# A decoder layer on one core: part of the weight and token sums of its seven-product groups move from accumulating DMAs and VectorE to GpSimd adds

## The chip, the core and the metric

One core of a Trainium2 chip runs the whole layer. The metric is the device time of one execution in microseconds; three executions of the kernel before gave 404.01, 404.17 and 405.35 us (median 404.17).

## What is computed

One decoder layer in float32 for 256 tokens of width 1024: a mixed attention block (block-sparse attention beside chunkwise retention), a cross-attention block over 256 memory rows, and a SwiGLU feed-forward block, each with RMS norms before and after. The change touches the last block alone:

```python
h = rms_norm(x, g_pre_ffn[l])
gu = h @ w_gate_up[l]
f = (jax.nn.silu(gu[..., :D_FF]) * gu[..., D_FF:]) @ w_down[l]
x = x + rms_norm(f, g_post_ffn[l])
```

`w_gate_up` is 1024 x 5632 and `w_down` 2816 x 1024.

## The kernel before

**Weights.** The host cuts all weights into blocks of 128 x 1024 floats (512 KB), here called quarters and numbered `q` in the order of their splitting. A quarter is loaded by one DMA of the SP queue into one of 5 `raw` buffers (L143). `split_weight` then splits it into two float32r matrices whose sum is the float32 value: ScalarE copies it rounded, the **high part** (L183), and VectorE subtracts that from the raw value, the **low part** (L184). TensorE multiplies with three products (high x high, high x low, low x high), for the operands on both sides are split so. Split quarters live in a ring of 9 `hl` buffers; while a quarter of the feed-forward stage finds no ring buffer free, `free_home` (L155) may also put it into the old activation tiles tagged "qv", "kT" and "ret": all three for the first 8 quarters of the stage, and after them "ret" alone.

**Order.** The program is written out step by step: a list `steps` of small groups of products sets TensorE's order, and after each step the loop emits what is due on the other engines: generators with waits counted in steps (table `WAIT`), and at most one split, once a home is free and, for a quarter that is a sum, at least `WAIT["sum"]` steps after the split of the value before it. Each engine works its own queue in that order.

**Seven-product groups.** Of the gate-up columns, two groups of 512 + 512 (`SEVEN = (2, 4)`, called group 2 and group 4) are computed as a 2 x 2 block product with seven products m1 to m7 instead of eight. The blocks are two token halves by two halves of the inner dimension, and B11, B12 (inner half 1, gate and up) and B21, B22 (inner half 2) for the weights. Each product takes two quarters. Its operands are sums: on the token side four sums per pair of inner blocks (`token_sums`, L602), made by VectorE from the normed tokens `x2T` (`xs`, `cs`: L612 to L619) and then split into `comb`; on the weight side sums that grow in place. In `seven_items` (L859) the tile `sum_kT` starts as B11 (weights of m1), becomes B11 + B12 (m5), + B22 (m6), + B21 (m4), and `sum_qv` starts as B22 (m3) and becomes B22 + B12 (m7). Each step on is an **accumulating DMA** of the GpSimd queue from the weights in HBM (L190), issued when the low part of the value before it has been read. The weights of m2, B21, are plain quarters. Between the seven products stand `down` products of earlier columns, one quarter each.

The quarters are used as `USE_ORDER` says: m1, d0, m2, d1, m5, d2, d3, m6, d4, m3, d5, m7, d6, m4, d7; they are split in the same order but for m3, which is split ahead of m6. In group 2 these are quarters 80 to 101: m1 is 80 and 81, m2 83 and 84, m5 86 and 87, m3 90 and 91, m6 92 and 93, m7 96 and 97, m4 99 and 100, the rest `down` quarters. Group 4 begins at 110 in the same way.

**After the products** (`seven_done`, L645): ScalarE copies the accumulators of m1, m5 and m6 (`s<-x`, `s<-y`); at m2 VectorE adds (`s<-z`, L651) and ScalarE applies silu (L653); at m3 VectorE computes `s<-y` (L656) and `s<-s` (L657), and two steps later TensorE transposes the result (`c_f`, L637) for the `down` products that follow.

Of the kernel before, what the change touches and what calls it, by code (L numbers as in the profile page):

```python
# [7 lines left out]
F32 = mybir.dt.float32  # L8
# [14 lines left out]
FFN_Q = 64  # L23
# [15 lines left out]
}  # L39
WARM = 9  # L40
# [7 lines left out]
def tile_hybrid_layer(  # L48
# [14 lines left out]
    nc = tc.nc  # L63
# [50 lines left out]
    T = {}  # L114
# [16 lines left out]
    items = [("w", q) for q in range(FFN_Q)]  # L131
    queue = []
    sums = {}
# [17 lines left out]
    homes = {}  # L151
# [2 lines left out]

    def free_home(q, i):  # L155

        if q in aside and last_use[homes["ret"]] + WAIT["lag"] <= i:
            return "ret"
        if len(ringed) < RING or last_use[ringed[-RING]] + WAIT["lag"] <= i:
            return "hl"  # L160
        if q >= FFN_Q and ("oT", 7, 1) in emitted:
            for tag in ("qv", "kT", "ret") if q < FFN_Q + 8 else ("ret",) if not any(q < a <= q + 6 for a in aside) else ():
                if tag not in homes or last_use[homes[tag]] + WAIT["lag"] <= i:
                    return tag
        return None

    def split_weight(q, parts=1, home="hl"):
        kind = items[q][0]
        if kind == "w":
            raw = raws.pop(q)  # L170
        else:
            g, tag, part = items[q][2:5]
            raw = sums[(g, tag)][:, part, :]
        if home == "hl":
            ringed.append(q)
            h = hlp.tile([P, 2, D], F32R, tag="hl", name=f"hl{q}")
        else:
            homes[home] = q
            h = actp.tile([P, 2, D], F32R, tag=home, name=f"hl{q}")
        w = D // parts  # L180
        for i in range(parts):
            n = slice(i * w, (i + 1) * w)
            nc.scalar.activation(h[:, 0, n], raw[:, n], AF.Copy)  # L183
            nc.vector.tensor_tensor(out=h[:, 1, n], in0=raw[:, n], in1=h[:, 0, n].bitcast(F32), op=ALU.subtract)  # L184
        hls[q] = h
        split_at[q] = step_no[0]
        if kind != "w":
            more = items[q][5]
            if more is not None:
                nc.gpsimd.dma_start(raw, weights[more], accum_op=ALU.add)  # L190
        if kind == "w":
            load_weight()

# [409 lines left out]
    def token_sums():  # L603

        T["comb"] = [(pt4 if i < 3 else p4).tile([P, 2, 4, P], F32R, tag="pt4" if i < 3 else "p4", name=f"comb{i}")
                     for i in range(4)]
        for i in range(4):
            need(*[("x2T", 2 * i + e, t) for e in range(2) for t in range(2)])
            x = tmp2k(f"xs{i}")
            pair = x.rearrange("p (e m) -> p e m", e=2)  # L610
            ks = slice(2 * i, 2 * i + 2)
            nc.vector.tensor_tensor(out=pair, in0=T["x2T"][:, 0, ks, :].bitcast(F32), in1=T["x2T"][:, 1, ks, :].bitcast(F32),  # L612
                                    op=ALU.add)
            c = tmp2k(f"cs{i}")
            nc.vector.tensor_tensor(out=c[:, 0:256].rearrange("p (e m) -> p e m", e=2),
                                    in0=x[:, 0:256].rearrange("p (e m) -> p e m", e=2), in1=pair[:, :, P:256],
                                    op=ALU.subtract)
            nc.vector.tensor_tensor(out=c[:, 256:384], in0=c[:, 128:256], in1=x[:, 0:P], op=ALU.subtract)
            nc.vector.tensor_tensor(out=c[:, 384:512], in0=c[:, 256:384], in1=x[:, 256:384], op=ALU.add)  # L619
            yield WAIT["ts0"]  # L620
            hi_lo(T["comb"][i][:, 0].rearrange("p c m -> p (c m)"), T["comb"][i][:, 1].rearrange("p c m -> p (c m)"), c)
            emitted.add(f"comb{i}")
            yield WAIT["ts1"]
# [235 lines left out]
    def seven_items(g, w0):  # L859

        b = {"11": w0, "12": w0 + 2, "21": w0 + 4, "22": w0 + 6}
        chain = {1: ("first", "11", "kT", "12"), 5: ("sum", "", "kT", "22"), 6: ("sum", "", "kT", "21"),
                 4: ("sum", "", "kT", None), 3: ("first", "22", "qv", "12"), 7: ("sum", "", "qv", None)}
        made = {}
        for m in range(1, 8):
            for part in range(2):
                if m == 2:
                    made[(m, part)] = ("w", b["21"] + part)
                else:
                    kind, w, home, more = chain[m]  # L870
                    made[(m, part)] = (kind, b[w] + part if w else None, g, home, part,
                                       None if more is None else b[more] + part)
        return made

    def seven_step(g, m, part, q):
# [1 line left out]
        begin = part == 0 and m in (1, 2, 5)  # L877
        steps.append(("seven", q, g, m, part, acc, begin))

    aside = set()  # L880
    for j in range(1, 5):
        if j not in SEVEN:
            gu_plain(range(4 * j, 4 * j + 4))
# [4 lines left out]
        made = seven_items(j, take(8)[0])  # L888
# [24 lines left out]
    last_use, first_use = {}, {}  # L913
# [6 lines left out]
    after = {}  # L920
    for q, item in enumerate(items):
        if item[0] == "sum":
            after[q] = max(p for p in range(q) if items[p][0] != "w" and items[p][2:5] == item[2:5])


    nc.gpsimd.memset(mhalf, -0.5)
# [11 lines left out]
    qv = actp.tile([P, 2048], F32, tag="qv", name="qv")  # L938
# [14 lines left out]
    nc.sync.dma_start(xr[0][:, 1, :], gx[:, 288:544])  # L953
    nc.sync.dma_start(raws[1][:, 512:1024], weights[1, :, 512:1024])
    nc.sync.dma_start(xr[0][:, 2:4, :], gx[:, 544:1056].rearrange("p (k m) -> p k m", k=2))
    queue[:] = [q for q in range(2, len(items)) if items[q][0] != "sum"]
    load_weight()
    load_weight()
    nc.sync.dma_start(xr[1], gx[:, 1056:2080].rearrange("p (k m) -> p k m", k=4))
# [49 lines left out]
    raw = raws.pop(0)  # L1009
# [19 lines left out]
    for i, s in enumerate(steps):  # L1029
# [17 lines left out]
        if s[0] == "first":  # L1047

            _, q, c = s
# [8 lines left out]
        elif s[0] == "col":  # L1058
            _, q, t, st, kp, key, first, last, done = s
# [15 lines left out]
        elif s[0] == "row":  # L1075
            _, q, half, st, nt, done = s
# [23 lines left out]
        elif s[0] == "down":  # L1100
            _, q, t, j, kk, halves = s
# [169 lines left out]
```

## Time and profile before

| | |
|---|---|
| three executions | 404.01, 404.17, 405.35 us (median 404.17) |
| the profiled execution | 404.76 us, of it 403.0 us span |
| granted TensorE clock | 0.997 |
| busy: TensorE / VectorE / ScalarE / GpSimd | 394.1 / 290.3 / 248.8 / 25.3 us |
| the chain that ended last | TensorE 71%, issue 9%, VectorE 6%, DMA 6%, ScalarE 4%, GpSimd 2% |
| DMA | 82.46 MB, mean 205 GB/s |
| feed-forward stage in the span | from about 215 us; group 2 from 261 to 304, group 4 from 326 to 368 |

The profile is of one execution. Engines are named PE (TensorE), PEld (its weight loads), DVE (VectorE), ACT (ScalarE), POOL (GpSimd), SP; a line L184 is that of the kernel before. A product's busy time overlaps the next one's, so TensorE's load is read from the distance of starts and from the idle time in brackets, not from its busy share. What an engine waits for matters where TensorE waits behind it.

### The profile page before, as it was taken

The numbers are of one execution on the slowest core, as the hardware profiler recorded it, in microseconds if no ns is written. First come the engines' busy times: TensorE is split into PE (matmuls) and PEld (weight loads), VectorE is DVE, ScalarE is ACT, GpSimd is POOL, SyncE is SP. The second block draws the span as 40 slices with busy tenths as digits, with TensorE's granted clock in tenths as the row PEclk, the third lists the DMA queues.
The fourth block names the chain that finished last, engine by engine and source line by source line (L and its number), as shares of the span: only waits on it lengthen the run. The fifth ranks groups of instructions, "written<-read, shape, count | busy, mean of one in ns | idle before, by whom it ended". The sixth has DMA issues, their size and how long they took to land.

```text
span 403.0 us, 5622 instructions
## 1 busy us (share of the span) xinstructions
PE 394.1 (98%) x2041; PEld 330.5 (82%) x2041; DVE 290.3 (72%) x435; ACT 248.8 (62%) x437; POOL 25.3 (6%) x37
## 2 busy tenths in 40 slices
PE   9999999999999999999999999999999999999993
PEld 5887777888888888988888888888788888878882
DVE  4885965776789977586656888888577667676732
ACT  5776883955667766485556865567365666664620
POOL 0010100200010000000011001013000103100000
PEclk9999999999999999999999999999999999999998
DMA  8998754387547676425354686989949798958011
GB/s 289 413 338 251 265 187 168 104 251 269 184 137 227 193 214 198 158 74 189 113 201 156 183 279 194 308 180 200 264 134 337 191 333 175 236 181 293 11 54 52
DMA packets 23499, 82.46 MB, mean 205 GB/s; under 512 B 2608, under 2 KB 2864, under 8 KB 23472
## 3 DMA queue, kind: packets, MB, share of 16 engines
q1 hardware_dynamic: 21024, 73.46, 53.5%
q0 software_dynamic: 2304, 8.39, 11.7%
q8 instruction: 16, 0.26, 0.3%
q10 hardware_dynamic: 144, 0.26, 0.2%
q14 instruction: 11, 0.09, 0.1%
HBM read 81.05 MB, written 1.05 MB: 204 GB/s over the span
## 4 chain that ended last, share of the span: by engine, by line
PE 71%; issue 9%; DVE 6%; DMA 6%; ACT 4%; POOL 2%; POOLq 0%; DVEq 0%; ACTq 0%
PE acc L1093 13%; PE acc L1069 10%; PE acc L1071 10%; PE acc L1070 10%; PE acc L1096 7%; DMA sum_kT<-in_weights_dram 6%; PE x L1129 3%; DVE hl L184 3%; PE acc L1057 3%; ACT hl L183 2%; PE down L1116 2%; PE down L1114 2%; PE down L1115 2%; PE warm L937 1%; ACT p_m L295 1%
## 5 line engine op out<-in xcount | busy, mean ns | idle before, releaser
L184 DVE TENSOR_TENSOR hl<-raw,hl 128x1024 fp32r<-128x1024 f32 (+1 forms) x120 | 140.7, 1194 | 25.3 <-ACT hl L183 24.9
L183 ACT ACTIVATE hl<-raw 128x1024 fp32r<-128x1024 f32 (+1 forms) x120 | 120.7, 1034 | 1.3 <-DMA raw<-in_weights_dram 1.2
L1093 PE MATMUL acc<-x2T,hl 128*128 128x512 f32 x160 | 39.2, 392 | 0.0
L1114 PE MATMUL down<-hl,fT 128*128 128x512 f32 x88 | 34.2, 389 | 0.0
L1115 PE MATMUL down<-hl,fT 128*128 128x512 f32 x88 | 34.2, 389 | 0.0
L1116 PE MATMUL down<-hl,fT 128*128 128x512 f32 x88 | 34.2, 389 | 0.0
L1093 PEld LDWEIGHTS acc<-x2T,hl 128*128 128x128 f32 x160 | 29.3, 188 | 5.5
L1069 PE MATMUL acc<-hl,xT 128*128 128x512 f32 x80 | 32.9, 411 | 0.0
L1071 PE MATMUL acc<-hl,xT 128*128 128x512 f32 x80 | 31.3, 391 | 0.0
L1070 PE MATMUL acc<-hl,xT 128*128 128x512 f32 x80 | 31.2, 391 | 0.0
L184 DVE TENSOR_TENSOR hl<-sum_kT,hl 128x1024 fp32r<-128x1024 f32 x16 | 19.4, 1224 | 9.6 <-ACT hl L183 9.6
L183 ACT ACTIVATE hl<-sum_kT 128x1024 fp32r<-128x1024 f32 x16 | 16.6, 1053 | 9.3 <-DMA sum_kT<-in_weights_dram 9.3
L1096 PEld LDWEIGHTS acc<-x2T,hl 128*128 128x128 f32 x160 | 20.6, 191 | 0.8
L1096 PE MATMUL acc<-x2T,hl 128*128 128x256 f32 x160 | 21.0, 283 | 0.0
L1116 PEld LDWEIGHTS down<-hl,fT 128*128 128x128 f32 x88 | 16.5, 188 | 3.5
L1115 PEld LDWEIGHTS down<-hl,fT 128*128 128x128 f32 x88 | 16.5, 188 | 3.5
L1114 PEld LDWEIGHTS down<-hl,fT 128*128 128x128 f32 x88 | 16.5, 188 | 3.4
L1071 PEld LDWEIGHTS acc<-hl,xT 128*128 128x128 f32 x80 | 15.0, 188 | 3.3
L1069 PEld LDWEIGHTS acc<-hl,xT 128*128 128x128 f32 x80 | 15.1, 189 | 3.2 <-issue 0.3
L1070 PEld LDWEIGHTS acc<-hl,xT 128*128 128x128 f32 x80 | 15.1, 189 | 2.6
L190 POOL DMA_DIRECT2D sum_kT<-in_weights_dram x12 | 10.7, 889 | 96.9 <-DVE hl L184 70.2
L518 ACT ACTIVATE fT<-sg 128x256 fp32r<-128x256 f32 x10 | 4.2, 418 | 19.7 <-DVE sg L598 19.7
(243 smaller groups left out, 805.9 us busy)
## 6 DMA issues: line engine op xcount, KB each, us to landing
raw<-in_weights_dram SPq DMA_DIRECT2D x116, 512.0 KB, 4.5
sum_kT<-in_weights_dram POOLq DMA_DIRECT2D x12, 512.0 KB, 7.6
sum_kT<-in_weights_dram SPq DMA_DIRECT2D x4, 512.0 KB, 6.0
sum_qv<-in_weights_dram SPq DMA_DIRECT2D x4, 512.0 KB, 6.8
sum_qv<-in_weights_dram POOLq DMA_DIRECT2D x4, 512.0 KB, 7.4
gpost<-in_gpost_dram SPq DMA_DIRECT2D x3, 512.0 KB, 5.1
x_sb<-in_x_dram SPq DMA_DIRECT2D x2, 512.0 KB, 6.9
memn<-in_mem_dram SPq DMA_DIRECT2D x2, 512.0 KB, 7.2
```

The source lines that it names most:

```text
L183: nc.scalar.activation(h[:, 0, n], raw[:, n], AF.Copy)
L184: nc.vector.tensor_tensor(out=h[:, 1, n], in0=raw[:, n], in1=h[:, 0, n].bitcast(F32), op=ALU.subtract)
L1057: nc.tensor.matmul(accs[(c, t)], T["xT"][:, hx, q, tok(t)], h[:, hw, :], start=begin, stop=False)
L1069: nc.tensor.matmul(acc, xh, h[:, 0, kk, :], start=(first and kk == 0), stop=False)
L1070: nc.tensor.matmul(acc, xh, h[:, 1, kk, :], start=False, stop=False)
L1071: nc.tensor.matmul(acc, xl, h[:, 0, kk, :], start=False, stop=(last and kk == 1))
L1093: nc.tensor.matmul(acc, hls[q][:, 0, k * P:(k + 1) * P], T[f"{st}_k"][:, k, :], start=begin, stop=end, skip_group_check=True)
L1096: nc.tensor.matmul(acc[:, 0:256], hls[q][:, 1, k * P:(k + 1) * P], T[st][:, 0, k, :], start=begin, stop=end, skip_group_check=True)
L1114: nc.tensor.matmul(acc, fh, wh, start=first, stop=False, skip_group_check=True)
L1115: nc.tensor.matmul(acc, fh, wl, start=False, stop=False, skip_group_check=True)
L1116: nc.tensor.matmul(acc, fl, wh, start=False, stop=last, skip_group_check=True)
L1129: nc.tensor.matmul(acc, a, h[:, w, kk, :], start=begin and kk == 0 and n == 0, stop=end and n == 2, skip_group_check=True)
```

## The change

`seven_items` gives each sum quarter three more fields. `plus` names a tile that GpSimd adds in place to `sum_kT` after the split (a 128 x 1024 `tensor_tensor`); `more` and `into` name the weights that an accumulating DMA adds, and the tile. m2's B21 is now loaded into a sum tile of its own, under the tag "ret", and split from there; it is never changed, for m4 adds it. So in each group B12 still comes by accumulating DMA twice (m5, m7), and B22 and B21 are now added by GpSimd (m6, m4): 4 adds and 4 accumulating DMAs per group in place of 8 such DMAs. "ret" is no longer a home for split quarters past the first 8 of the stage. The four instructions of each token sum move from VectorE to GpSimd, and their waits in `WAIT` change.

```diff
-    ... "ts0": 1, "ts1": 7, ...
+    ... "ts0": 3, "ts1": 4, ...
...
     def free_home(q, i):
-        if q in aside and last_use[homes["ret"]] + WAIT["lag"] <= i:
-            return "ret"
         if len(ringed) < RING or last_use[ringed[-RING]] + WAIT["lag"] <= i:
             return "hl"
         if q >= FFN_Q and ("oT", 7, 1) in emitted:
-            for tag in ("qv", "kT", "ret") if q < FFN_Q + 8 else ("ret",) if not any(q < a <= q + 6 for a in aside) else ():
+            for tag in ("qv", "kT", "ret") if q < FFN_Q + 8 else ():
...
         if kind != "w":
-            more = items[q][5]
+            plus, more, into = items[q][5:8]
+            if plus is not None:
+                total = sums[(g, "kT")][:, part, :]
+                nc.gpsimd.tensor_tensor(out=total, in0=total, in1=sums[(g, plus)][:, part, :], op=ALU.add)
             if more is not None:
-                nc.gpsimd.dma_start(raw, weights[more], accum_op=ALU.add)
+                nc.gpsimd.dma_start(sums[(g, into)][:, part, :], weights[more], accum_op=ALU.add)
...
-            nc.vector.tensor_tensor(out=pair, in0=T["x2T"][:, 0, ks, :].bitcast(F32), in1=T["x2T"][:, 1, ks, :].bitcast(F32),
+            nc.gpsimd.tensor_tensor(out=pair, in0=T["x2T"][:, 0, ks, :].bitcast(F32), in1=T["x2T"][:, 1, ks, :].bitcast(F32),
...
-            nc.vector.tensor_tensor(out=c[:, 0:256].rearrange("p (e m) -> p e m", e=2),
+            nc.gpsimd.tensor_tensor(out=c[:, 0:256].rearrange("p (e m) -> p e m", e=2),
...
-            nc.vector.tensor_tensor(out=c[:, 256:384], in0=c[:, 128:256], in1=x[:, 0:P], op=ALU.subtract)
-            nc.vector.tensor_tensor(out=c[:, 384:512], in0=c[:, 256:384], in1=x[:, 256:384], op=ALU.add)
+            nc.gpsimd.tensor_tensor(out=c[:, 256:384], in0=c[:, 128:256], in1=x[:, 0:P], op=ALU.subtract)
+            nc.gpsimd.tensor_tensor(out=c[:, 384:512], in0=c[:, 256:384], in1=x[:, 256:384], op=ALU.add)
...
-        chain = {1: ("first", "11", "kT", "12"), 5: ("sum", "", "kT", "22"), 6: ("sum", "", "kT", "21"),
-                 4: ("sum", "", "kT", None), 3: ("first", "22", "qv", "12"), 7: ("sum", "", "qv", None)}
+        chain = {1: ("first", "11", "kT", None, "12", "kT"), 2: ("first", "21", "ret", None, None, None),
+                 3: ("first", "22", "qv", None, "12", "qv"), 4: ("sum", None, "kT", None, None, None),
+                 5: ("sum", None, "kT", "qv", None, None), 6: ("sum", None, "kT", "ret", None, None),
+                 7: ("sum", None, "qv", None, None, None)}
```

(`aside` was an empty set.) The products and their order on TensorE are the same. On the other engines the order moves at these places; in the names the first number is the quarter's (`hl86`), or group and token half (`s6_2`).

VectorE about the m5 quarters of group 2 (86 and 87), before and then changed:

```order
L519 TENSOR_TENSOR fT_2182<-sg6_2542,fT_2182 128x256
L585 TENSOR_TENSOR sg7_2597<-acc157_2570,sg7_2597 128x256
L184 TENSOR_TENSOR hl86_2611<-sum_kT2_2330,hl86_2611 128x1024
L595 TENSOR_TENSOR sg7_2597<-acc159_2600,sg7_2597 128x256
L184 TENSOR_TENSOR hl87_2631<-sum_kT2_2330,hl87_2631 128x1024
L612 TENSOR_TENSOR xs3_2641<-x2T_1939 128x512
L615 TENSOR_TENSOR cs3_2643<-xs3_2641 128x256
L618 TENSOR_TENSOR cs3_2643<-cs3_2643,xs3_2641 128x128
L619 TENSOR_TENSOR cs3_2643<-cs3_2643,xs3_2641 128x128
L598 TENSOR_TENSOR sg7_2597<-sg7_2597 128x256
L519 TENSOR_TENSOR fT_2182<-sg7_2597,fT_2182 128x256
L519 TENSOR_TENSOR comb3_2312<-cs3_2643,comb3_2312 128x512
```

```order
L586 TENSOR_TENSOR sg7_2591<-acc157_2566,sg7_2591 128x256
L182 TENSOR_TENSOR hl85_2611<-raw85_2363,hl85_2611 128x1024
L596 TENSOR_TENSOR sg7_2591<-acc159_2594,sg7_2591 128x256
L182 TENSOR_TENSOR hl86_2632<-sum_kT2_2328,hl86_2632 128x1024
L520 TENSOR_TENSOR comb3_2312<-cs3_2607,comb3_2312 128x512
L599 TENSOR_TENSOR sg7_2591<-sg7_2591 128x256
L520 TENSOR_TENSOR fT_2182<-sg7_2591,fT_2182 128x256
L182 TENSOR_TENSOR hl87_2657<-sum_kT2_2328,hl87_2657 128x1024
L182 TENSOR_TENSOR hl88_2669<-raw88_2380,hl88_2669 128x1024
L182 TENSOR_TENSOR hl89_2681<-raw89_2406,hl89_2681 128x1024
L652 TENSOR_TENSOR s1_2_2647<-z2_2674,s1_2_2647 128x512
```

Token sum 3 (`xs3`, `cs3`) is gone, `hl86` stands where `hl87` stood, behind `sg7<-acc159`, and `hl87` behind `sg7<-sg7` and `fT`. ScalarE at the same place, before and then changed:

```order
L183 ACTIVATE hl86_2611<-sum_kT2_2330 128x1024
L593 ACTIVATE sg7_2597<-acc159_2600 128x256
L587 ACTIVATE sg7_2597<-sg7_2597 128x256
L183 ACTIVATE hl87_2631<-sum_kT2_2330 128x1024
L518 ACTIVATE fT_2182<-sg7_2597 128x256
L648 ACTIVATE s1_2_2650<-x2_2622 128x512
L518 ACTIVATE comb3_2312<-cs3_2643 128x512
L183 ACTIVATE hl88_2662<-raw88_2402 128x1024
```

```order
L594 ACTIVATE sg7_2591<-acc159_2594 128x256
L588 ACTIVATE sg7_2591<-sg7_2591 128x256
L181 ACTIVATE hl86_2632<-sum_kT2_2328 128x1024
L519 ACTIVATE comb3_2312<-cs3_2607 128x512
L519 ACTIVATE fT_2182<-sg7_2591 128x256
L649 ACTIVATE s1_2_2647<-x2_2623 128x512
L181 ACTIVATE hl87_2657<-sum_kT2_2328 128x1024
L181 ACTIVATE hl88_2669<-raw88_2380 128x1024
```

The high part of `hl86` stands behind `sg7<-sg7`, where that of `hl87` stood, and `hl87` now stands behind `fT` and `s1_2<-x2`, the copy of m1's accumulator.

VectorE ahead of the transposes `c_f2_0`, before and then changed:

```order
L184 TENSOR_TENSOR hl96_2766<-sum_qv2_2518,hl96_2766 128x1024
L184 TENSOR_TENSOR hl97_2775<-sum_qv2_2518,hl97_2775 128x1024
L184 TENSOR_TENSOR hl98_2784<-raw98_2582,hl98_2784 128x1024
L184 TENSOR_TENSOR hl99_2803<-sum_kT2_2330,hl99_2803 128x1024
L656 TENSOR_TENSOR s6_2_2795<-y2_2719,s6_2_2795 128x512
L657 TENSOR_TENSOR s6_2_2795<-s6_2_2795,s1_2_2650 128x512
L184 TENSOR_TENSOR hl100_2832<-sum_kT2_2330,hl100_2832 128x1024
L640 TENSOR_TENSOR fT_2182<-c_f2_0_2841,fT_2182 128x4x128
L184 TENSOR_TENSOR hl101_2854<-raw101_2665,hl101_2854 128x1024
```

```order
L182 TENSOR_TENSOR hl96_2771<-sum_qv2_2435,hl96_2771 128x1024
L182 TENSOR_TENSOR hl97_2780<-sum_qv2_2435,hl97_2780 128x1024
L182 TENSOR_TENSOR hl98_2797<-raw98_2614,hl98_2797 128x1024
L657 TENSOR_TENSOR s6_2_2789<-y2_2714,s6_2_2789 128x512
L658 TENSOR_TENSOR s6_2_2789<-s6_2_2789,s1_2_2647 128x512
L182 TENSOR_TENSOR hl99_2828<-sum_kT2_2328,hl99_2828 128x1024
L641 TENSOR_TENSOR fT_2182<-c_f2_0_2837,fT_2182 128x4x128
L182 TENSOR_TENSOR hl100_2850<-sum_kT2_2328,hl100_2850 128x1024
```

`hl99`, m4's first quarter, stood ahead of `s6_2<-y2` and `s6_2<-s6_2`, which `c_f2_0` transposes, and now stands behind them.

GpSimd in group 2, before (with the last operation ahead of it and the first of group 4) and then changed:

```order
L202 TENSOR_TENSOR r_p_cross1_2176<-v_p_cross1_2174,mhalf_101 128x1
L202 TENSOR_TENSOR r_x21_2194<-v_x21_2192,mhalf_101 128x1
L190 DMA sum_kT2_2330<-in_weights_dram 128x1024 x4
L190 DMA sum_qv2_2518<-in_weights_dram 128x1024 x2
L190 DMA sum_kT2_2330<-in_weights_dram 128x1024 x2
L190 DMA sum_kT4_2917<-in_weights_dram 128x1024 x4
```

```order
L191 DMA sum_kT2_2328<-in_weights_dram 128x1024 x2
L613 TENSOR_TENSOR xs2_2506<-x2T_1939 128x512
L616 TENSOR_TENSOR cs2_2508<-xs2_2506 128x256
L619 TENSOR_TENSOR cs2_2508<-cs2_2508,xs2_2506 128x128
L620 TENSOR_TENSOR cs2_2508<-cs2_2508,xs2_2506 128x128
L613 TENSOR_TENSOR xs3_2605<-x2T_1939 128x512
L616 TENSOR_TENSOR cs3_2607<-xs3_2605 128x256
L619 TENSOR_TENSOR cs3_2607<-cs3_2607,xs3_2605 128x128
L620 TENSOR_TENSOR cs3_2607<-cs3_2607,xs3_2605 128x128
L189 TENSOR_TENSOR sum_kT2_2328<-sum_kT2_2328,sum_qv2_2435 128x1024 x2
L191 DMA sum_qv2_2435<-in_weights_dram 128x1024 x2
L189 TENSOR_TENSOR sum_kT2_2328<-sum_kT2_2328,sum_ret2_2360 128x1024 x2
```

Each row of two is a pair of parts, one for each quarter. Adds 1 and 2 (`sum_kT2<-sum_kT2,sum_qv2`) stand behind the splits of 86 and 87, adds 3 and 4 (`...,sum_ret2`) behind those of 92 and 93 and behind the two DMAs into `sum_qv2`.

## Rows read from the trace of the kernel before

**Rows 1.** The page, busy time, share of the span and instructions of TensorE:

```profile
PE 394.1 (98%) x2041; PEld 330.5 (82%) x2041; DVE 290.3 (72%) x435; ACT 248.8 (62%) x437; POOL 25.3 (6%) x37
```

**Rows 2.** TensorE's timeline in the two seven-product groups: start us, duration us, engine, line, operation, output<-inputs, columns, count, and in brackets the idle time before and what ended it:

```profile
274.85 0.39 PE L1114 MATMUL down<-hl,fT 128*128 128x512 f32 x1
...
277.56 0.39 PE L1114 MATMUL down<-hl,fT 128*128 128x512 f32 x1
...
280.29 2.88 PE L1129 MATMUL x<-hl,comb 128*128 128x512 f32 x12
283.00 0.39 PE L1114 MATMUL down<-hl,fT 128*128 128x512 f32 x1
...
290.71 0.39 PE L1115 MATMUL down<-hl,fT 128*128 128x512 f32 x1
290.94 0.39 PE L1116 MATMUL down<-hl,fT 128*128 128x512 f32 x1
292.18 0.66 PE L637 MATMUL c_f<-cst,s 128*128 128x128 f32 x4 [0.85 <-DVE s L657]
...
356.01 0.39 PE L1116 MATMUL down<-hl,fT 128*128 128x512 f32 x1
356.77 0.66 PE L637 MATMUL c_f<-cst,s 128*128 128x128 f32 x4 [0.37 <-DVE s L657]
```

**Rows 3.** The list of who waited for whom: engine, what, line <- releaser: us in total, times, longest us:

```profile
PEld c_f L637 <- DVE s L657: 2.1, 2, 1.3
```

**Rows 4.** VectorE's timeline in group 2 (columns as in Rows 2; `hl` is a low part, `s` the m1 to m3 arithmetic):

```profile
264.78 1.23 DVE L184 TENSOR_TENSOR hl<-sum_kT,hl 128x1024 fp32r<-128x1024 f32 x1
...
270.50 2.36 DVE L184 TENSOR_TENSOR hl<-raw,hl 128x1024 fp32r<-128x1024 f32 x2 [0.26 <-ACT hl L183]
...
277.38 2.35 DVE L184 TENSOR_TENSOR hl<-sum_kT,hl 128x1024 fp32r<-128x1024 f32 x2
279.65 2.35 DVE L184 TENSOR_TENSOR hl<-raw,hl 128x1024 fp32r<-128x1024 f32 x2
...
289.57 1.23 DVE L184 TENSOR_TENSOR hl<-sum_kT,hl 128x1024 fp32r<-128x1024 f32 x1 [0.75 <-ACT hl L183]
290.71 0.68 DVE L656 TENSOR_TENSOR s<-y,s 128x512 f32<-128x512 f32 x1
291.43 0.69 DVE L657 TENSOR_TENSOR s<-s,s 128x512 f32<-128x512 f32 x1
```

**Rows 5.** ScalarE's timeline in group 2 (columns as in Rows 2; `hl` is a high part):

```profile
263.69 1.06 ACT L183 ACTIVATE hl<-sum_kT 128x1024 fp32r<-128x1024 f32 x1
268.09 0.42 ACT L518 ACTIVATE fT<-sg 128x256 fp32r<-128x256 f32 x1 [3.34 <-DVE sg L598]
268.42 0.58 ACT L648 ACTIVATE s<-x 128x512 f32<-128x512 f32 x1
...
274.63 0.63 ACT L653 ACTIVATE s<-s 128x512 f32<-128x512 f32 x1 [2.27 <-DVE s L651]
...
288.48 1.06 ACT L183 ACTIVATE hl<-sum_kT 128x1024 fp32r<-128x1024 f32 x1 [0.62 <-DMA sum_kT<-in_weights_dram]
```

**Rows 6.** The timeline early in the stage, VectorE's row (low parts of quarters 76 to 78) and TensorE's (the first products of quarter 72):

```profile
237.47 3.50 DVE L184 TENSOR_TENSOR hl<-raw,hl 128x1024 fp32r<-128x1024 f32 x3
...
238.54 1.98 PE L1093 MATMUL acc<-x2T,hl 128*128 128x512 f32 x8
```

**Rows 7.** Groups of VectorE instructions by line and shape from 226 to 270 us, the four kinds of a token sum: line, engine, operation, names, shapes, count | busy us, mean ns | idle us before:

```profile
L612 DVE TENSOR_TENSOR xs<-x2T 128x512 f32<-128x512 f32 x4 | 2.7, 686 | 0.0
...
L615 DVE TENSOR_TENSOR cs<-xs 128x256 f32<-128x256 f32 x4 | 1.7, 425 | 0.1
...
L618 DVE TENSOR_TENSOR cs<-cs,xs 128x128 f32<-128x128 f32 x4 | 1.2, 293 | 0.1
L619 DVE TENSOR_TENSOR cs<-cs,xs 128x128 f32<-128x128 f32 x4 | 1.2, 292 | 0.1
```

**Rows 8.** The page, DMA issues: names, queue, count, KB each, median us from issue to landing:

```profile
sum_kT<-in_weights_dram POOLq DMA_DIRECT2D x12, 512.0 KB, 7.6
```

**Rows 9.** Timeline (columns as in Rows 2): GpSimd's small operations and the VectorE operations beside them:

```profile
48.89 1.22 DVE L184 TENSOR_TENSOR hl<-raw,hl 128x1024 fp32r<-128x1024 f32 x1
48.99 1.52 POOL L202 TENSOR_TENSOR r_mem<-v_mem,mhalf 128x1 f32<-128x1 f32 x1 [25.86 <-DVE v_mem L198]
...
119.56 1.12 DVE L502 SCALAR_TENSOR_TENSOR x1T<-xt_mix,xg,x1T 128x128 fp32r<-128x128 f32 x4
119.73 0.55 POOL L202 TENSOR_TENSOR r_x<-v_x,mhalf 128x1 f32<-128x1 f32 x1 [4.78 <-DVE v_x L198]
...
124.75 0.41 DVE L519 TENSOR_TENSOR ckl<-kf,ckh 128x256 fp32r<-128x256 f32 x1
124.91 0.66 POOL L202 TENSOR_TENSOR r_x<-v_x,mhalf 128x1 f32<-128x1 f32 x1 [4.63 <-DVE v_x L198]
```

**Rows 10.** The timeline in group 4 (columns as in Rows 2): VectorE's two m5 quarters, then TensorE's starts:

```profile
331.67 2.36 DVE L184 TENSOR_TENSOR hl<-sum_kT,hl 128x1024 fp32r<-128x1024 f32 x2 [1.01 <-ACT hl L183]
...
342.64 0.39 PE L1114 MATMUL down<-hl,fT 128*128 128x512 f32 x1
...
345.36 2.88 PE L1129 MATMUL x<-hl,comb 128*128 128x512 f32 x12
348.08 0.39 PE L1114 MATMUL down<-hl,fT 128*128 128x512 f32 x1
```

More of the change, by code (lines that the diff above doesn't have):

```diff
@@ L861, in seven_items @@
         b = {"11": w0, "12": w0 + 2, "21": w0 + 4, "22": w0 + 6}
-        chain = {1: ("first", "11", "kT", "12"), 5: ("sum", "", "kT", "22"), 6: ("sum", "", "kT", "21"),
-                 4: ("sum", "", "kT", None), 3: ("first", "22", "qv", "12"), 7: ("sum", "", "qv", None)}
+        chain = {1: ("first", "11", "kT", None, "12", "kT"), 2: ("first", "21", "ret", None, None, None),
+                 3: ("first", "22", "qv", None, "12", "qv"), 4: ("sum", None, "kT", None, None, None),
+                 5: ("sum", None, "kT", "qv", None, None), 6: ("sum", None, "kT", "ret", None, None),
+                 7: ("sum", None, "qv", None, None, None)}
         made = {}
-        for m in range(1, 8):
+        for m, (kind, source, home, plus, more, into) in chain.items():
             for part in range(2):
[L867 to L872, printed above, removed]
+                made[(m, part)] = (kind, b[source] + part if source else None, g, home, part, plus,
+                                   None if more is None else b[more] + part, into, m)
         return made
@@ L878, in seven_step @@
         steps.append(("seven", q, g, m, part, acc, begin))
-    aside = set()
     for j in range(1, 5):
@@ L922, in tile_hybrid_layer @@
         if item[0] == "sum":
-            after[q] = max(p for p in range(q) if items[p][0] != "w" and items[p][2:5] == item[2:5])
+            after[q] = max(p for p in range(q) if items[p][0] != "w" and items[p][2] == item[2]
+                           and items[p][4] == item[4] and items[p][3] == item[3])
     nc.gpsimd.memset(mhalf, -0.5)
@@ L955, in tile_hybrid_layer @@
     nc.sync.dma_start(xr[0][:, 2:4, :], gx[:, 544:1056].rearrange("p (k m) -> p k m", k=2))
-    queue[:] = [q for q in range(2, len(items)) if items[q][0] != "sum"]
+    queue[:] = [q for q in range(2, len(items)) if items[q][0] in ("w", "first")]
     load_weight()
```

2 rows, old and new, of the table WAIT are left out of this document.

## The prediction

> **What bounds the kernel now.** I read first the page's busy line: TensorE stands at 394.1 of 403.0 us [rows 1]. Then TensorE's own timeline, for holes. In the feed-forward part its products stand back to back, 0.227 us apart, but for two places [rows 2]: the last product before the transposes of `c_f` starts at 290.94 and the transposes at 292.18 instead of 291.17, and in the second seven-product group at 356.77 instead of 356.24. Those 1.01 and 0.53 us are all that faster feeding can win there. The list of waits names the same place: 2.1 us before `c_f`, ended by VectorE's `s` [rows 3]. Why `s` was late stands on the timelines of VectorE [rows 4] and ScalarE [rows 5]: `s<-y` stands behind the low part of an m4 quarter (289.57), whose high part on ScalarE (288.48) waited for the accumulating DMA, and the second `s` ended at 292.12.
>
> Then I read how early a quarter's low part ends on VectorE against TensorE's first use of it. Early in the stage there is room: the third of the rows at 237.47, quarter 78, ends at 240.97, and TensorE, which starts quarter 72 at 238.54 and needs some 2.8 us for each, comes to it near 255 [rows 6]. Late in the first group (group 2) there is little: m6's first quarter ends at 278.6 and is used at 280.29, the next `down` quarter ends at 280.87 and is used at 283.00 [rows 2, 4]. A delay of VectorE of over 2 us between 264 and 281 reaches TensorE.
>
> **The change, part by part.**
>
> *Removed from VectorE:* 16 token-sum instructions, 2.7 + 1.7 + 1.2 + 1.2 = 6.8 us [rows 7]. Three of the four sums lie where quarters are 8 to 15 us early, which hides them; the fourth is in the tight stretch, and the walk below leaves it out.
>
> *Removed from the DMA queues:* 8 of 16 accumulating DMAs, a median of 7.6 us each to landing [rows 8]. What they delay is ScalarE's m4 high parts. In the new order `s<-y` stands ahead of the first m4 quarter, so the two holes lose their cause: up to -1.01 - 0.53 = -1.54.
>
> *The home of its own:* m2's quarters no longer come through the raw buffers, and "ret" no longer takes split quarters. In the new order m5's first quarter takes the place that its second had (ScalarE 263.69, VectorE 264.78 to 266.00), and its second falls behind `s<-x`: 1.5 us less room, which the walk holds.
>
> *Added on GpSimd:* 8 adds of 128x1024, and the 16 token-sum instructions. Two questions: how long is an add, and what does VectorE do meanwhile? On the second the trace has rows. A one-column GpSimd operation takes 0.55 us, as at 119.73, beside VectorE operations that read PSUM. The one that began at 48.99 took 1.52 and ended 0.41 after VectorE's low part of 48.89, which has two inputs in SBUF; the one at 124.91 took 0.66 and ended 0.41 after another such operation (124.75, 0.41 long) [rows 9]. So GpSimd waits for the end of a VectorE operation with two SBUF inputs. I take it that the wait holds the other way too: for the length of an add, VectorE starts no low part. [...] The trace agrees on GpSimd's side (1.52 against 0.55); no row here shows VectorE waiting, so the opposite is a rival.
>
> The length of an add has no row. Lower end: one pass of VectorE, 1.14 us (two low parts in 2.36, less 1.22 [rows 4]). Upper end: three passes, 3.4, if both operands and the result went one after the other. I take two passes, 2.3: what GpSimd waited for is something that VectorE's operations need only with a second SBUF input, so both operands of an add would have to come through that one door. [...]
>
> *The token sums on GpSimd* also block VectorE, but while quarters are 8 to 15 us early [rows 6]: nothing; without that cover, about 2.3 us for each.
>
> **Walk of group 2**, on the clock of before: low parts 1.14 apart, the last 0.08 longer, the port to whoever asked first. m5's first quarter ends 266.0 and the `comb` low part behind it (0.6) 266.6; add 1 holds the port to 268.9; `sg` (0.4) 269.3. ScalarE does `fT`, `s<-x` and the high part of m5's second quarter (0.42, 0.58, 1.06, overlapping by 0.1), so that quarter ends at 272.5 and the next, a `down` quarter, at 273.7 (needed 274.85). Add 2 to 276.0; the next `down` quarter 277.2 (needed 277.56); `s<-z` (0.68) 277.9. ScalarE's 0.63 and a high part of 1.04 stand ahead of m3's first quarter, which starts at 279.6; two m3 quarters and m6's first end at 283.1, needed at 280.29: **2.8 late**. m6's second 284.2, in time by now; add 3 to 286.5; the `down` quarter behind it 287.7, needed at 283.0 + 2.8: **1.9 more**. Add 4 to 290.0; four quarters to 294.6; `s<-y` and `s` (1.4) to 296.0, needed at 291.17 + 4.7: 0.1 more. Lost 4.8 in place of 1.0: **+3.8**.
>
> **Walk of group 4** [rows 10], where the order keeps its places: m5's second quarter ends 334.0; add 1 to 336.3; the `down` quarter 337.5; add 2 to 339.8 (`s<-z` reads PSUM and passes); the next `down` quarter 341.0 (needed 342.64); two m3 quarters and m6's first to 344.5 (345.36), its second 345.7; add 3 to 348.0; the `down` quarter 349.2, needed at 348.08: 1.1 late. Add 4 to 351.5; four quarters to 356.1; `s` 357.5, needed at 356.24 + 1.1: 0.2 more. Lost 1.3 in place of 0.5: **+0.8**.
>
> **The sum.** +3.8 + 0.8 = +4.6 us on the profiled execution's 404.76, so 409.4; that execution stands 0.6 above the median of 404.17, against which I give **408.8 us**. Each group has four adds in its path, so upward from here 0.1 us on an add is 0.8 us on the kernel: with 3.4 it is +13.4. With 1.14 the late quarters of group 2 cost 0.5 and 0.7, group 4 none, and both holes at `c_f` close: 1.2 - 1.54 = -0.3.
>
> **Rivals.** (a) *VectorE does not stop for GpSimd* (ends faster). Then its low parts come no more than 1.5 us later, and the fourth token sum's 1.7 us earlier; both holes close, and the sum is -1.54: 402.6. For it: no row shows VectorE waiting. Against: GpSimd waited to the end of the other's operation, so the door is held, not shared. It decides at the first add, near 266.6: if the `sg` operation behind it starts at once, this is the case. (b) *Short adds*, 1.14 to 1.9 us, or a block for part of one: the delays are of the holes' size, 403.5 to 405.4. (c) *Long adds*, 2.7 to 3.4 us, by a start cost on GpSimd that holds the door too (its smallest operation takes 0.55 [rows 9]): 412 to 417.6. (d) *The accumulating DMAs that are left*: m7's quarters still come by DMA behind m3's low parts. In the walk those end by 282, and with 0.9 to issue and 7.6 to land the sums are there near 290.5, while VectorE comes to them at 291; it decides nothing, and in (a) all of it is 2 to 3 us earlier. It has no price of its own.
>
> **How the numbers follow.** Forecast (adds of 2.0 to 2.65 us that block) 0.52, with a range of its own of 406.4 to 411.6; (c) 0.10; (b) 0.12; (a) 0.26. What a measurement of this kernel can tell from no change is about 0.3%, 1.2 us: faster 0.26, same 0.12, slower 0.62. The range holds the forecast, (b) and (a) and leaves out (c): 402.4 to 411.6.
>
> **What would show it.** In the changed profile: adds near 2.3 us, longer where they begin beside a low part; a `sg` operation held up by some 2 us beside add 1; TensorE waiting at `x` (m6) and at the `down` products behind it, some 5 us in group 2 and 1 in group 4, and next to nothing at `c_f`. Low parts that keep their 1.22 us and start while an add runs, with both holes gone, would make the forecast wrong in favour of (a). Adds of 1.2 us would make it (b).

## The result and the profile after

The changed kernel takes **409.28 us** (median of 4 runs, 408.10 to 409.77), the kernel before 404.59 (4 runs, 404.01 to 405.35): a ratio of **1.0111** (95% interval 1.0081 to 1.0140), 4.7 us slower. The forecast was 408.8, slower, in a range of 402.4 to 411.6. The profiled execution took 408.10, the lowest of the four, with a span of 406.3; the profiled one of the kernel before took 404.76, with a span of 403.0.

The page's busy line, which answers to [rows 1]:

```profile
PE 396.3 (98%) x2041; PEld 331.1 (81%) x2041; DVE 302.9 (75%) x419; ACT 248.4 (61%) x437; POOL 60.7 (15%) x53
```

VectorE has 16 instructions fewer and is busy 12.6 us longer: its operations have grown. The list of waits of TensorE (PE) and of its weight loads (PEld) shows where that arrives (engine, what, line <- releaser: us in total, times, longest us):

```profile
PE x L1128 <- ACT hl L181: 1.3, 1, 1.3
PE x L1128 <- DVE hl L182: 1.1, 1, 1.1
...
PEld c_f L638 <- DVE s L658: 0.5, 2, 0.2
...
PE down L1114 <- DVE hl L182: 0.3, 1, 0.3
```

At `c_f` no product waits any more, and the weight loads of [rows 3] wait 0.5 us in place of 2.1; `x` is m6. The same on TensorE's timeline, for the starts of [rows 2] (280.29, 283.00, 292.18, 356.77):

```profile
280.05 0.39 PE L1115 MATMUL down<-hl,fT 128*128 128x512 f32 x1
281.70 0.50 PE L1128 MATMUL x<-hl,comb 128*128 128x512 f32 x1 [1.26 <-ACT hl L181]
283.34 4.15 PE L1128 MATMUL x<-hl,comb 128*128 128x512 f32 x11 [1.14 <-DVE hl L182]
287.30 0.63 PE L1113 MATMUL down<-hl,fT 128*128 128x512 f32 x1
...
295.91 0.62 PE L638 MATMUL c_f<-cst,s 128*128 128x128 f32 x4
...
352.43 0.50 PE L1114 MATMUL down<-hl,fT 128*128 128x512 f32 x1 [0.30 <-DVE hl L182]
...
360.54 0.62 PE L638 MATMUL c_f<-cst,s 128*128 128x128 f32 x4
```

The second product of m6 starts at 283.34, where it stood at 280.29 + 0.23: 2.8 late. The `down` product behind m6 starts 4.3 later than before, `c_f` 3.7 later (the hole of 1.0 there is gone), and the second group adds nothing in sum (3.8 later at its `c_f`).

GpSimd's timeline with the eight adds (three rows hold a pair each), then VectorE's beside them in group 2 and at the first pair of group 4:

```profile
266.88 2.77 POOL L189 TENSOR_TENSOR sum_kT<-sum_kT,sum_qv 128x1024 f32<-128x1024 f32 x1 [4.82 <-DVE hl L182]
273.16 3.30 POOL L189 TENSOR_TENSOR sum_kT<-sum_kT,sum_qv 128x1024 f32<-128x1024 f32 x1 [3.50 <-DVE hl L182]
...
283.37 6.62 POOL L189 TENSOR_TENSOR sum_kT<-sum_kT,sum_ret 128x1024 f32<-128x1024 f32 x2
...
336.64 6.67 POOL L189 TENSOR_TENSOR sum_kT<-sum_kT,sum_qv 128x1024 f32<-128x1024 f32 x2 [13.53 <-DVE hl L182]
...
347.99 6.64 POOL L189 TENSOR_TENSOR sum_kT<-sum_kT,sum_ret 128x1024 f32<-128x1024 f32 x2
```

```profile
266.72 0.68 DVE L520 TENSOR_TENSOR comb<-cs,comb 128x512 fp32r<-128x512 f32 x1
267.32 2.62 DVE L599 TENSOR_TENSOR sg<-sg 128x256 f32<-128x256 f32 x1
...
273.00 4.55 DVE L182 TENSOR_TENSOR hl<-raw,hl 128x1024 fp32r<-128x1024 f32 x2
...
284.34 6.74 DVE L182 TENSOR_TENSOR hl<-raw,hl 128x1024 fp32r<-128x1024 f32 x2
...
337.60 3.42 DVE L182 TENSOR_TENSOR hl<-raw,hl 128x1024 fp32r<-128x1024 f32 x1
340.95 0.68 DVE L652 TENSOR_TENSOR s<-z,s 128x512 f32<-128x512 f32 x1
```

Read the two side by side. Add 1 began at 266.88, while a `comb` low part ran to 267.40; it ended at 269.65, so it had the door (the prediction's word for what only one of the two engines can use at a time) for 2.25 us of its 2.77. The `sg` operation behind that low part, 0.42 us elsewhere, took 2.62 and ended 0.29 after the add. A low part that is caught by an add takes 3.42 us instead of 1.22: **VectorE loses 2.2 us for each add**. In the pairs the two engines take turns: two low parts and two adds in 6.74. The `s<-z` at 340.95, which reads PSUM, kept its 0.68 while add 2 of the second group held the door.

### The profile page after: what moved, and what is told of

It is laid out like the page before. It is cut to its first block, busy times and chain, and to the rows that moved or that the text cites. A ratio compares the mean times of both kernels' runs of the same rounds, so it can differ in the third digit from the quotient of the medians.

```text
span 406.3 us, 5609 instructions
## 1 busy us (share of the span) xinstructions
PE 396.3 (98%) x2041; PEld 331.1 (81%) x2041; DVE 302.9 (75%) x419; ACT 248.4 (61%) x437; POOL 60.7 (15%) x53
## 4 chain that ended last, share of the span: by engine, by line
PE 77%; DVE 10%; issue 6%; ACT 4%; POOL 2%; DVEq 0%; POOLq 0%; ACTq 0%
PE acc L1092 14%; PE acc L1068 11%; PE acc L1070 11%; PE acc L1069 11%; PE acc L1095 7%; DVE hl L182 6%; PE x L1128 4%; PE acc L1056 3%; PE down L1114 3%; PE down L1115 2%; PE down L1113 2%; ACT hl L181 2%; PE y L1128 1%; PE warm L936 1%; DVE sg L599 1%
## 5 line engine op out<-in xcount | busy, mean ns | idle before, releaser
L182 DVE TENSOR_TENSOR hl<-raw,hl 128x1024 fp32r<-128x1024 f32 (+1 forms) x116 | 150.5, 1320 | 23.8 <-ACT hl L181 23.5
L181 ACT ACTIVATE hl<-raw 128x1024 fp32r<-128x1024 f32 (+1 forms) x116 | 116.6, 1034 | 2.0 <-DMA raw<-in_weights_dram 1.7
L1092 PE MATMUL acc<-memT,hl 128*128 128x512 f32 x64 | 16.3, 396 | 0.0
```

What stands on the lines that cost most here:

```text
L1092: nc.tensor.matmul(acc, hls[q][:, 0, k * P:(k + 1) * P], T[f"{st}_k"][:, k, :], start=begin, stop=end, skip_group_check=True)
```

## The experiments

The table shows, for every kernel run, by how much TensorE loses (+) or wins (-) against the profile of before at each place, as the starts of the same products on the two timelines show it. Shifts of 0.0 to 1.0 us that each profile already has at 50 us are taken off by setting the products at 200 us equal. A `c_f` column is read at the product behind `c_f`. The names are those of the experiments below.

| kernel | m6 and `down`, group 2 | `c_f`, group 2 | `down`, group 4 | `c_f`, group 4 | at the end |
|---|---|---|---|---|---|
| changed | +4.8 | -1.0 | +0.6 | -0.6 | +3.7 |
| adds_on_vector | +3.2 | -1.1 | +1.2 | -0.6 | +2.8 |
| adds_half | +1.5 | +0.1 | 0 | -0.6 | +1.0 |
| one_input | +0.7 | -0.3 | 0 | -0.6 | -0.2 |
| token_sums_back | +4.4 | -0.7 | +0.6 | -0.5 | +3.8 |
| dma_sums | 0 | -1.1 | 0 | -0.6 | -1.65 |
| first_two_adds | +3.0 | +0.8 | 0 | -0.6 | +3.15 |
| last_two_adds | +0.4 | -0.9 | 0 | -0.6 | -1.1 |
| adds_later | 0 | -0.6 | 0 | -0.6 | -1.3 |
| later_s_first | 0 | -1.1 | 0 | -0.6 | -1.67 |
| before_s_first | 0 | -1.1 | 0 | -0.6 | -1.67 |

The last one or two tenths of a row are drift between two profiles. The theory is that of the prediction: a GpSimd add and a VectorE operation with two SBUF inputs exclude each other. Its first rival: the new order and the new home make the quarters late, and the adds do not.

**1. The adds back to DMA, all else as changed** (dma_sums).

```
-  5: ("sum", None, "kT", "qv", None, None), 6: ("sum", None, "kT", "ret", None, None),
+  5: ("sum", None, "kT", None, "22", "kT"), 6: ("sum", None, "kT", None, "21", "kT"),
```

> The changed kernel with its 8 GpSimd adds turned back into accumulating DMAs; the home of its own, the new order and the token sums on GpSimd stay. Theory (the GpSimd adds alone make the loss, by keeping VectorE out): no hole at m6 nor at the down quarter behind it; at c_f in the first group 0 to 0.9 us is left (the sums of m7 still come by DMA), in the second none: 403.0 to 404.5 us. Rival (the new order makes quarters late): a hole of over 0.5 us at m6, 405.5 us or more.

Measured: 403.23 us, ratio 0.9958 (0.9934 to 0.9982): 1.5% under the changed kernel's median. No wait of TensorE is left in either group, and the products behind the first `c_f` start 1.06 us earlier than in the kernel before, those behind the second by another 0.58. So the adds alone make the loss; the new order and the home are innocent, and the order closes both holes, since `s<-y` now stands ahead of m4's first quarter (experiment 7 tries that alone, on the kernel before). The token sums are still on GpSimd here: they cost nothing.

**2. The token sums back on VectorE, the adds on GpSimd** (token_sums_back; four times `nc.gpsimd` to `nc.vector` in `token_sums`).

> The changed kernel with its 16 token-sum instructions back on VectorE; the weight adds stay on GpSimd. The prediction put the token sums at nothing in either place, since quarters are 8 to 15 us early there; the fourth sum, 1.7 us of VectorE near 257 to 262, could reach the tight stretch. Theory: as the changed kernel, 409.3 us (408.6 to 410.5), m6 late by 2.8 us or a little more. Rival (the token sums on GpSimd hold VectorE up enough to be felt): 407 to 408.4 us.

Measured: 409.12 us, ratio 1.0093 (1.0075 to 1.0111), m6 2.6 late, and 1.8 more at `down`. Together with experiment 1 this shows both halves of the prediction's zero. The token sums do hold VectorE up where they stand (a low part at 228.17 took 1.53 us, two at 230.94 took 3.64), but there the quarters are early.

**3. Half as long adds** (adds_half).

```
-  nc.gpsimd.tensor_tensor(out=total, in0=total, in1=sums[(g, plus)][:, part, :], op=ALU.add)
+  nc.gpsimd.tensor_tensor(out=total[:, 0:512], in0=total[:, 0:512],
+                          in1=sums[(g, plus)][:, part, 0:512], op=ALU.add)
```

> The changed kernel with each GpSimd add over 512 of its 1024 columns; the other half of the sum is left out. Port theory: what VectorE loses goes with the length of the add, some 1.2 to 1.3 us in place of 2.2 (a GpSimd sum of 512 columns took 1.29 us in the changed kernel); m6's first quarter is late by 2.8 - 2 x 0.95 = 0.9, low parts beside an add last some 2.4 instead of 3.4: 404.3 to 405.5 us. Rival (a fixed start cost of the add, or the new order, makes the loss): 407.5 us or more.

Measured: 405.58 us, just above the expected range, ratio 1.0004 (0.9989 to 1.0019). The loss goes with the length: m6 is late by 0.8 instead of 2.8. VectorE's timeline of this kernel:

```profile
282.93 4.55 DVE L182 TENSOR_TENSOR hl<-raw,hl 128x1024 fp32r<-128x1024 f32 x2
```

Two low parts between which two half adds came take 4.55 instead of 6.74, so a half add costs (4.55 - 2.36) / 2 = 1.1 us where a whole one costs 2.2. At `c_f` 0.9 us of waiting was left, which the expectation had not held; experiment 6 shows what that is.

**4. One SBUF input on GpSimd** (one_input).

```
-  nc.gpsimd.tensor_tensor(out=total, in0=total, in1=sums[(g, plus)][:, part, :], op=ALU.add)
+  nc.gpsimd.tensor_scalar(total, total, 0.0, None, op0=ALU.add)
```

> The changed kernel with each GpSimd add replaced by a GpSimd operation over the same 1024 columns that has one SBUF input (adding the constant 0 in place); the sum is left out. Narrow port theory (the door is held only by an operation with two SBUF inputs): the low parts keep 1.22 us beside it, TensorE has no hole at m6, and the two holes at c_f close too: 402.6 to 403.4 us. Wide theory (any GpSimd operation on SBUF keeps VectorE out for its length, or shares its rate): low parts beside it stay long, 406 to 409.5 us.

Measured: 404.94 us, ratio 0.9996 (0.9981 to 1.0010), between the two theories. GpSimd's timeline of this kernel, then VectorE's beside it:

```profile
267.53 3.15 POOL L189 TENSOR_SCALAR sum_kT<-sum_kT 128x1024 f32<-128x1024 f32 x1 [4.83 <-DVE hl L182]
272.45 3.69 POOL L189 TENSOR_SCALAR sum_kT<-sum_kT 128x1024 f32<-128x1024 f32 x1 [1.76 <-DVE hl L182]
```

```profile
267.96 1.26 DVE L599 TENSOR_TENSOR sg<-sg 128x256 f32<-128x256 f32 x1
269.70 0.43 DVE L520 TENSOR_TENSOR fT<-sg,fT 128x256 fp32r<-128x256 f32 x1 [0.48 <-ACT fT L519]
...
272.28 3.19 DVE L182 TENSOR_TENSOR hl<-raw,hl 128x1024 fp32r<-128x1024 f32 x2
```

Here GpSimd's operation is longer than an add (3.15 to 3.69 us) and holds VectorE up for only 0.83 (`sg` 1.26 for 0.42, two low parts 3.19 for 2.36). The `fT` low part at 269.70, with two SBUF inputs, ran its plain 0.43 while it went on. So how long GpSimd runs is not the measure, and the mere traffic does not give it either (one operand read and one written in place of two and one is two thirds, the hold 0.83 of 2.2): with two inputs VectorE was kept out for the whole add (2.2 of 2.25 us), with one for about a third of the operation (0.83 of 2.6, which is 3.15 less the 0.52 that it waited for a low part).

**5. The adds on VectorE, at the same places** (adds_on_vector; `nc.gpsimd` to `nc.vector` in the one line).

> The changed kernel with its 8 weight adds on VectorE in place of GpSimd, at the same places in the order; the token sums stay on GpSimd. Port theory (an add on GpSimd and a two-input SBUF operation of VectorE exclude each other, so that each add costs VectorE 2.2 us): an add costs VectorE only its own pass, about 1.15 us, so m6's first quarter, 2.8 us late behind two adds, is late by 2.8 - 2 x 1.05 = 0.7, the down quarter behind it by some 0.7 more, and nothing is left at c_f: about 404.3 us (403.5 to 405.5), adds of 1.1 to 1.3 us and no low part longer than 1.3. Rival (the new home and the new order make the quarters late, not GpSimd): 408.5 to 410, TensorE still waits over 2 us at m6.

Measured: 408.15 us, ratio 1.0070 (1.0054 to 1.0086). The adds are as short as expected, and the time is 4 us off, close to the rival's, which experiment 1 rules out. VectorE's timeline shows why:

```profile
281.15 1.22 DVE L182 TENSOR_TENSOR hl<-sum_kT,hl 128x1024 fp32r<-128x1024 f32 x1
282.40 1.23 DVE L189 TENSOR_TENSOR sum_kT<-sum_kT,sum_ret 128x1024 f32<-128x1024 f32 x1
283.54 1.22 DVE L182 TENSOR_TENSOR hl<-sum_kT,hl 128x1024 fp32r<-128x1024 f32 x1
284.80 1.23 DVE L189 TENSOR_TENSOR sum_kT<-sum_kT,sum_ret 128x1024 f32<-128x1024 f32 x1
285.94 2.35 DVE L182 TENSOR_TENSOR hl<-raw,hl 128x1024 fp32r<-128x1024 f32 x2
```

In VectorE's order an add stands exactly where it was written: adds 3 and 4 are both ahead of the `down` quarter (285.94), add 3 even ahead of m6's second. On GpSimd add 4 came only behind that quarter. So three adds of 1.15 to 1.25 lie in front of it from add 2 on, 3.6 us, against two of 2.2, 4.4 us: the cheaper adds still leave two thirds of the delay (3.2 of 4.8). My 404.3 took over the prediction's figure for short adds, which holds for adds that run beside.

**6. Which adds: the first two or the last two** (first_two_adds, last_two_adds; the other two by DMA, as in experiment 1, one entry each).

> The changed kernel with adds 3 and 4 of each group (m6's parts into m4's sum) turned back into accumulating DMAs; adds 1 and 2 stay on GpSimd. By the walk the first two adds alone make m6's first quarter late: 2.8 us in the first group, nothing at the down quarter behind it, nothing in the second group; both holes at c_f close, -1.06 and -0.58. Together +1.2 on the kernel before: 405.8 us (405.2 to 406.5). Rival (what counts is the number of adds, not the place): half of the changed kernel's loss at each place, m6 late by 1.4, about 404.7 us.

> The changed kernel with adds 1 and 2 of each group (the parts into m6's sum) turned back into accumulating DMAs; adds 3 and 4 stay on GpSimd. By the walk m6 is in time, add 3 holds the low part of the down quarter back by 2.2 us, some 1.7 of which it has to spare: 0.5 us late in the first group, nothing in the second; both holes at c_f close. Together -1.1: 403.5 us (403.1 to 404.4). Rival (by number, not by place): the down quarter 1.9 us late, 404.9 us.

Measured: the last two alone 403.47 us, ratio 0.9975 (0.9962 to 0.9988), the `down` quarter 0.4 late: as walked. The first two alone 407.72, ratio 1.0080 (1.0062 to 1.0099), above the expected range: m6 3.0 late as walked, nothing at `down`, but `c_f` does not close, it opens. ScalarE's and VectorE's timelines of that kernel in group 2, and TensorE's:

```profile
287.63 1.06 ACT L181 ACTIVATE hl<-sum_qv 128x1024 fp32r<-128x1024 f32 x1 [2.27 <-DMA sum_qv<-in_weights_dram]
291.15 1.06 ACT L181 ACTIVATE hl<-sum_qv 128x1024 fp32r<-128x1024 f32 x1 [2.46 <-DMA sum_qv<-in_weights_dram]
```

```profile
292.24 1.23 DVE L182 TENSOR_TENSOR hl<-sum_qv,hl 128x1024 fp32r<-128x1024 f32 x1 [2.29 <-ACT hl L181]
293.68 1.23 DVE L182 TENSOR_TENSOR hl<-raw,hl 128x1024 fp32r<-128x1024 f32 x1 [0.20 <-ACT hl L181]
294.82 0.69 DVE L657 TENSOR_TENSOR s<-y,s 128x512 f32<-128x512 f32 x1
```

```profile
296.29 0.66 PE L638 MATMUL c_f<-cst,s 128*128 128x128 f32 x4 [1.62 <-DVE s L658]
```

m7's sums still come by DMA, issued only when m3's low parts are done. What delays m3 delays that transfer, its second part lands at 291.1, and `s<-y` stands behind the m7 quarters. In the changed kernel the same transfer lands at 290.5, and adds 3 and 4 bring VectorE to m7's second quarter at 292.14 anyway. The two ways to `s` tie within 0.3 us there, and taking one away shows the other: behind `c_f` both kernels stand 3.7 to 3.8 us late (4.8 - 1.0 and 3.0 + 0.8), so the 1.8 us that adds 3 and 4 put in at the `down` quarter are not paid on top. This transfer is also what is left at `c_f` in adds_half (0.9) and one_input (0.6).

**7. A version that beats both.** Two edits follow from this. The adds on VectorE, but in its idle stretches: add 1 ahead of m5's second low part, add 2 ahead of m3's first, adds 3 and 4 ahead of the two m7 low parts:

```
-  nc.gpsimd.tensor_tensor(out=total, in0=total, in1=sums[(g, plus)][:, part, :], op=ALU.add)
+  adds.append((sums[(g, "kT")][:, part, :], sums[(g, plus)][:, part, :]))
...
   nc.scalar.activation(h[:, 0, n], raw[:, n], AF.Copy)
+  if kind != "w" and (items[q][8], part) in ((5, 1), (3, 0), (7, 0), (7, 1)):
+      total, extra = adds.pop(0)
+      nc.vector.tensor_tensor(out=total, in0=total, in1=extra, op=ALU.add)
```

And `s<-y` ahead of the `down` quarter behind m7, by not splitting that quarter before the step of m3's second part:

```
+  if what[1] == 3:
+      not_before[place[("d", 6)]] = len(steps) - 1
...
-  if paced and home and not hold and (quiet or near):
+  if paced and home and not hold and (quiet or near) and i >= not_before.get(q, 0):
```

> The changed kernel with its adds on VectorE at four chosen places: add 1 ahead of m5's second low part and add 2 ahead of m3's first, where VectorE idles 1.0 and 1.65 us with the adds gone, adds 3 and 4 ahead of the two m7 low parts, where it waits for a DMA. Theory (the adds on VectorE cost where they stand, 3.6 us ahead of the down quarter, and not by their number): m6 and the down quarter in time but for 0.3 us, at c_f up to 0.9 us left in the first group: 403.2 to 404.6 us. Rival (8 more passes of VectorE do not fit into the stage at all): 406 to 408 us, as with the adds on VectorE at the old places.

> As adds_later, and the down quarter that stands between m7's second quarter and s<-y is held back until s<-y is issued. Theory: what is left at c_f goes, 402.5 to 403.4 us, faster than both kernels. Rival (m7's quarters by DMA still hold s up, or the held quarter is late itself): 403.5 to 404.6 us, with a wait at c_f or at the down quarter behind m7.

> The kernel before with one edit: the down quarter behind m7 is held back until s<-y is issued, so that s<-y and s<-s stand ahead of it and of m4's first quarter on VectorE; all sums by DMA as before. Theory (the holes at c_f, 1.01 and 0.53 us, come from m4's low part waiting for its DMA ahead of s): both go, 402.5 to 403.4 us. Rival (the same transfer then makes m4's quarter itself late, or m7's does it at c_f): 403.8 to 404.8 us.

Measured: adds_later 403.97, ratio 0.9969 (0.9944 to 0.9993); later_s_first 403.38, 0.9963 (0.9946 to 0.9980); before_s_first, the kernel before with the second edit alone, **403.23**, 0.9962 (0.9942 to 0.9983). The eight passes of VectorE that ended 2.8 us behind the kernel before at their old places delay no product of TensorE in the gaps, but for 0.4 us at `c_f` in adds_later, which the second edit removes. VectorE's timeline of later_s_first, with an add in each gap, 0.52 us of idle time left of 1.65, and `s<-y` now waiting for TensorE's products instead of being waited for:

```profile
268.72 1.22 DVE L185 TENSOR_TENSOR sum_kT<-sum_kT,sum_qv 128x1024 f32<-128x1024 f32 x1
...
273.86 1.21 DVE L185 TENSOR_TENSOR sum_kT<-sum_kT,sum_qv 128x1024 f32<-128x1024 f32 x1
275.60 1.23 DVE L186 TENSOR_TENSOR hl<-sum_qv,hl 128x1024 fp32r<-128x1024 f32 x1 [0.52 <-ACT hl L182]
...
289.19 0.69 DVE L660 TENSOR_TENSOR s<-y,s 128x512 f32<-128x512 f32 x1 [1.06 <-PE y L1134]
```

The three fastest kernels (with dma_sums) all stand at -1.65 to -1.67 in the table and do not differ by more than their intervals: in both groups TensorE has no hole left, so nothing more is to be won there.

## Why the prediction was right, step by step

- **GpSimd and VectorE exclude each other, both ways**: shown. What only GpSimd's rows told before holds on VectorE's side too: a low part takes 3.42 for 1.22, and what VectorE loses for each add halves with half adds (1.1 us for 2.2), and the whole loss goes with the adds gone (403.23 us; experiments 1, 3). That the door goes to whoever asked first, as the walk has it (there it is the port), the prediction assumed for VectorE's side; the changed profile shows it at add 1, which began at 266.88 beside the `comb` low part and had the door from 267.40, ahead of the `sg` operation of 267.32, which ended at 269.94. Rival (a) is refuted. Its price of -1.54 was right for a VectorE that is not held up (dma_sums, without the adds: -1.65). Where it was held up by 0.83 us for each operation (one_input) the result was -0.2: +0.7 at m6 and `down`, and at `c_f` -0.3 in place of -1.1, because of m7's transfer.
- **The add's length**: taken as two passes, 2.3; measured 2.25 (2.77 less 0.52 of waiting) and 2.2 of VectorE's time. Rivals (b) and (c) fall with it. That two operands make two passes was the author's estimate, and no run shows it: the operation with one took 2.6 (experiment 4).
- **The walk of group 2**: m6's first quarter was to be 2.8 late, the `down` quarter's low part to end at 287.7, m7's and the next `down` quarter's by 294.6, `s` at 296.0. Measured on the changed timeline, whose products stand at the same times as before's up to there: 2.8, 287.74, 294.49 and 295.81. Net of the hole at `c_f` the group costs 3.7, forecast 3.8. A small error cancelled: m6's first low part ended at 283.29 (walked 283.1), and TensorE needs a low part only for the second product of a quarter, 0.23 later than the walk has it.
- **The 1.9 us at the `down` quarter** came in another form. In this profile TensorE arrived there late by itself, because its granted clock stood at 0.50 for 3.41 us after the hole (last section); in token_sums_back, where it had not, the wait stood at `down` as forecast (1.8 us), and at `c_f` the two are the same, +3.7 and +3.8.
- **The walk of group 4** was too dear by 0.8 in sum: 1.3 late was forecast, 0.6 measured, and the hole of 0.6 closed, so that the group costs nothing. The low part of the `down` quarter ended at 352.38, which is 348.7 on the clock of before (3.66 less); the walk had 349.2, against a need of 348.08. It had gathered 0.5 us over the quarters and adds ahead of it (m6's second quarter was put at 345.7 and ended at 345.4 on that clock), and the need, by the second product again, was 0.23 later, in a place with only 0.5 to 1 us to decide, and the second delay of 0.2 behind it fell away with that.
- **The sum**: +4.6 forecast; +3.7 on TensorE's timeline. The medians differ by 4.7, the two profiled executions by 3.3; the interval of the medians reaches from 3.3 to 5.7, and single profiles stand up to 1 us apart before the stage that was changed. So that 408.8 lies so near 409.28 is partly luck; the mechanism and the main term were right, the term of group 4 was not.
- **Rival (d)**, the transfers that are left, "decides nothing": true in the changed kernel by 0.3 us only, and false in first_two_adds, adds_half and one_input. It deserved a price: where the adds cost less, it sets the end. So the prediction's -0.3 for adds of 1.14 us was wrong: the half adds, which hold VectorE up for 1.1 us, cost 1.5 at m6 and `down` (forecast 1.2), but the hole at `c_f` of group 2 stayed, and the sum was +1.0.
- **The token sums at nothing and the holes at `c_f` closed**: as forecast (experiments 1 and 2).

## What to carry to other kernels

An elementwise operation that was moved to GpSimd was not off VectorE here, where both read two SBUF operands: each add took 2.2 us from VectorE, while the same add on VectorE took 1.15 to 1.25. What it costs then depends on where it falls: eight passes made the kernel 2.8 us later at one set of places in VectorE's order, and no product waited for them in its idle gaps once `s<-y` stood first too (later_s_first), so look for the gaps first and choose the engine after. And a stall that is removed is worth only the way down to the next late thing: price that one too, even where it decides nothing in the case at hand.

## What the runs showed of the hardware that was not expected

TensorE's granted clock fell after the 2.8 us hole at m6 in the changed kernel's profile: m6's products from 284.7 to 286.9 stand 0.43 us apart instead of 0.23. The profile's clock stands at 0.50 from 284.45 to 287.86, 3.41 us, and at 1.00 on both sides. The windows of 283 to 288 us, first of the changed kernel, then of token_sums_back and first_two_adds, with holes of 2.5 and 2.85 us at the same place (columns: stretch, length, busy us and counts by engine, TensorE's clock, DMA share, GB/s):

```profile
283.00:288.00 5.00, 4.66 (x13) 3.32 (x14) 5.00 (x4) 2.83 (x4) 5.00 (x3) 0.66 1.00 176
```

```profile
283.00:288.00 5.00, 3.04 (x13) 2.20 (x13) 5.00 (x4) 2.25 (x4) 5.00 (x3) 1.00 0.99 170
```

```profile
283.00:288.00 5.00, 4.28 (x19) 3.55 (x20) 4.07 (x4) 2.73 (x4) 2.60 (x3) 1.00 0.94 155
```

So behind a hole of about the same size the clock fell in one execution (0.66 in the mean of these 5 us) and not in two others (1.00 in both). What decides it was not shown. The fall cost next to nothing in this place, since the low part of the quarter behind it ended at 287.74, when TensorE had just come to it.

The other surprise is the one-input GpSimd operation of experiment 4: longer than the two-input add over the same columns (2.6 against 2.25 us without the waiting), and yet VectorE was held up by it for 0.83 us only. Why that is so was not tried.
